# Low halves of three first projections, and differences of neighbouring tokens, on VectorE instead of GpSimd

## The chip, the cores and the metric

The kernel runs on one core of one Trainium2 chip. The metric is the device time of one execution in microseconds (us). Before the change it was 2815.28 us, the median of 3 runs (2813.53 to 2815.95).

Five engines work side by side, each through a queue of its own in order: TensorE (PE in the profile; its weight loads are PEld), VectorE (DVE), ScalarE (ACT), GpSimd (POOL) and SyncE (SP), which here issues nearly all transfers (DMA).

## The reference

A trunk of two layers on 1024 tokens of width 1024, in float32. Layer 0 is windowed and dilated attention with a gated MLP; layer 1 is an RWKV-7 time mix with a gated MLP. The change lies at the start of the time mix:

```python
xx = jnp.pad(h[:, :-1], ((0, 0), (1, 0), (0, 0))) - h
xr, xw, xk, xv, xa, xg = [h + xx * mu[i] for i in range(6)]
r = xr @ w_rkv[0]
k = xk @ w_rkv[1]
v = xv @ w_rkv[2]
w = -jax.nn.softplus(-(w0 + jnp.tanh(xw @ w1) @ w2)) - 0.5
...
a = jax.nn.sigmoid(a0 + (xa @ a1) @ a2)
g = jax.nn.sigmoid(xg @ g1) @ g2
```

`xx` is the difference between a token and the one before it, the six `x?` are the mixes. Decay `w`, rate `a` and gate `g` each go through a narrow first projection (`w1`, `a1`, `g1`) and a second one.

## The kernel before, in words

**Two halves of a number.** PE multiplies in a rounded type, fp32r. To keep float32 accuracy every operand is split: the high half is the operand cast to fp32r (ACT), the low half is the operand minus its high half (a subtraction). A product is then three matmuls: high by high, high by low, low by high (`mm3`, lines 180 to 182). `split` (line 154) does cast and subtraction, the subtraction on DVE unless it is told otherwise.

**Tiling.** Tokens go in two halves of 512 (the loop over `q` in `rwkv_dense`), the 1024 channels in 8 blocks of 128 partitions (`k`). A tile is 128 channels by 512 tokens. `hT[k]` holds the normed activations, channels on partitions, with one column more at the front for the token before.

**The stage that the change touches.** For each half:

- line 1144 makes the 8 differences `xx` from two shifted views of `hT[k]`: for even `k` on DVE, for odd `k` on POOL;
- `mix` (line 1149) makes a mixed tile on DVE with one instruction, `xx * mu + h`;
- `mixed` makes the mixes for values (`xv`), receptance (`xr`) and keys (`xk`) and splits them with `split`: tiles `xi`, both halves by ACT and DVE;
- `lora1` does a first projection. It loads its weights (`lw`), splits them (lines 1176 and 1177), and then for each `k` makes a mix into a tile `s`, `u` or `sq` (DVE), casts it (line 1187, ACT) and makes the low half (line 1188, POOL), into a ring of three slots: two under the tag `tm` (`xl` in the profile) and one under `na`. Then come its matmuls into `pg` (gate) or `psi` (decay, rate). Gate comes first, then decay, then rate: 24 mixes per half;
- in the same loop over `ch` and `k` the value product runs: weights `wv` are loaded (`raw`), split (`wh` on ACT, `wl` on DVE; in half 1 `wl` comes back from DRAM, line 170), and multiplied with `xv` into `pv`. So the first projections are woven into the value product, three steps of `lora1` for two of `k`;
- then the gate's `rb` is finished (ACT, POOL, DVE), `pv` is copied to `u` and `sq` and stored (`v_d`), the second weights are split (`w`, `a`, `g2s`), the gate's second projection runs (`pz`, line 1286, stored as `gT`), and a loop over 8 blocks of columns `c` makes keys and receptance and all that follows from them.

The tag `tm` is also used at the end of that loop over `c`, for tiles that are stored as `bm_d` and `km_d`; so the first `xl` of half 1 wait for the last of these stores.

**What sets the order.** The order of instructions within a queue isn't that of the code. The kernel is built with

```python
with tile.TileContext(nc, schedule_with_timeline_sim=True) as tc:
```

which plans the order of every engine ahead of time from planned durations of its own. Once built, the order is fixed, and each engine takes its instructions strictly one behind the other; an instruction that waits for another engine holds up what is queued behind it. An edit that gives an instruction to another engine therefore also changes the planned order of others.

Of the kernel before, what the change touches and what calls it, by code (L numbers as in the profile page):

```python
# [11 lines left out]
F32 = mybir.dt.float32  # L12
# [7 lines left out]
ADD, SUB, MUL, MAX = ALU.add, ALU.subtract, ALU.mult, ALU.max  # L20
# [7 lines left out]
H = 512  # L28
# [1022 lines left out]
def rwkv_dense(t, hp, sv, hT, first):  # L1051

    tc, nc, a, dp = t.tc, t.nc, t.a, t.dp
    ve, ac, po, pe = nc.vector, nc.scalar, nc.gpsimd, nc.tensor
# [81 lines left out]
    for q in range(2):  # L1136
# [4 lines left out]
        for k in range(NK):  # L1141
            if k % 2 == 0:
                x2 = (sv, sv, up, up)[k // 2].tile([P, 2, H], F32, name="xx", tag=("n", "ub", "bk", "ar")[k // 2], bufs=(1, 1, 2, 2)[k // 2])
            (po if k % 2 else ve).tensor_tensor(x2[:, k % 2], hT[k][:, q * H:(q + 1) * H], hT[k][:, 1 + q * H:1 + (q + 1) * H], SUB)
            xx.append(x2[:, k % 2])

        def mix(i, k, tag):
            x = tile_(tag)
            ve.scalar_tensor_tensor(x, xx[k], t.v(f"mu{i}", k), hT[k][:, 1 + q * H:1 + (q + 1) * H], MUL, ADD)
            return x  # L1150
# [8 lines left out]
        def lora1(i, name, halves, *parts):  # L1159

            n = a[name].shape[1] // NK
            per = (256 if name == "a1" else 512) // n
            raw = wp.tile([P, NK * n], F32, name="lw", tag="lw", bufs=1)
            nc.sync.dma_start(raw, a[name])
            raw = raw.rearrange("p (k c) -> p k c", k=NK)
            ws = []  # L1170
            for k0 in range(0, NK, per):
                kn = min(per, NK - k0)
                w = next(halves)[:, :kn * 2 * n].rearrange("p (k c) -> p k c", k=kn)
                for c0, m, _ in parts:
                    src, wh, wl = raw[:, k0:k0 + kn, c0:c0 + m], w[:, :, 2 * c0:2 * c0 + m], w[:, :, 2 * c0 + m:2 * c0 + 2 * m]
                    ac.copy(wh, src)
                    ve.tensor_tensor(wl, src, wh.bitcast(F32), SUB)
                ws += [w[:, k] for k in range(kn)]
            for k in range(NK):
                x = mix(i, k, ("s", "u", "sq")[k % 3])  # L1180
                tag = next(rings)
                if tag == "tm":
                    xs = tp.tile([P, 2, H], F32R, name="xl", tag=tag)
                    xs = xs[:, 0], xs[:, 1]
                else:
                    xs = [tile_(tag, dt=F32R) for _ in range(2)]
                ac.copy(xs[0], x)
                po.tensor_tensor(xs[1], x, xs[0].bitcast(F32), SUB)
                for c0, m, ps in parts:
                    w = ws[k][:, 2 * c0:2 * c0 + 2 * m]  # L1190
                    if m > 64:
                        t.mm3(ps, w[:, :m], w[:, m:], *xs, k == 0, k == NK - 1)
                    else:
                        for j in (0, 1) if k == 0 else (1, 0):
                            mj = m if j else 2 * m
                            pe.matmul(ps[:mj], w[:, :mj], xs[j], start=k == j == 0, stop=k == NK - 1 and not j)
                yield

        def product(i, xi, c):
            wh, wl = t.load_split(wp, a["wrk"][i, c], D, "w", 2, lo=po if i == 0 and not q else ve, **through(wrkl[i, c]))  # L1200
            ps = pm.tile([P, H], F32, name="pz", tag="mm")
            for k in range(NK):
# [11 lines left out]
        a1s = (tile_("xx", dt=F32R) for _ in range(2))  # L1214
        rings = itertools.cycle(["tm", "tm", "na"])
        parts = itertools.chain(lora1(5, "g1", slots, (0, P, pga), (P, 32, pgb)),
                                lora1(1, "w1", w1s, (0, 64, psw)), lora1(4, "a1", a1s, (0, 64, psa)))
        xrs = []
        for ch in range(2):
# [437 lines left out]
def trunk(tc, a, out):  # L1657
    with ExitStack() as ctx:
        t = Trunk(ctx, tc, a, out)
        x_m, x_d, x_l = (t.dp.tile([T, D], F32, name=n) for n in ("x_m", "x_d", "x_l"))  # L1660
        hp = ctx_pool(tc, "hp", "left")
        mp = ctx_pool(tc, "mp", "left")
        o, merge = t.attention(hp.pool, mp.pool)
        up = t.ffn_up(0, "left", "right")
        mt = ctx_pool(tc, "mt", "left")
        r = t.out_proj("right", o, a["wout"], a["x"], x_m, None, 0, functools.partial(merge, mt.pool),
                       lambda: (mt.close(), mp.close(), next(up), next(up)))
        act = up.send((*r, hp))
        hp = ctx_pool(tc, "hr", "left")
        rn = ctx_pool(tc, "rn", "left", 2)  # L1670
        hT, done = rwkv_norm(t, hp.pool, rn.pool, x_d)
        t.ffn_down(0, act, x_m, "right", done)
        rn.close()
        sv = ctx_pool(tc, "sv", "right")
        d, scan, last = rwkv_dense(t, hp, sv.pool, hT, Scan)
        o, op, behind = rwkv_scan(t, d, scan, sv, last)
        scan.lp.close()
        ow = ctx_pool(tc, "ow", "right")
        up = t.ffn_up(1, "right", "left")
        next(up)  # L1680
        r = t.out_proj("left", o, a["wo"], x_d, x_l, ow, 1, None, lambda: next(up), behind)
        act = up.send((*r, op, ow))
        zn = ctx_pool(tc, "zn", "right", 2)
        t.ffn_down(1, act, x_l, "left", t.final(zn.pool))
        zn.close()
# [23 lines left out]
```

## Time and profile before

| what | value |
| --- | --- |
| median of 3 runs | 2815.28 us |
| the profiled execution's own time | 2819.46 us |
| its span (first to last instruction) | 2817.7 us |
| mean granted TensorE clock | 0.963 |
| differences `xx` (line 1144), DVE x8, median | 977 ns |
| differences `xx` (line 1144), POOL x8, median | 1453 ns |
| low halves (line 1188), POOL | 48 instructions, medians by group 1340 to 1750 ns |
| mixes (line 1149), DVE | 96 instructions, medians by group 740 to 751 ns, longest 2367 ns |
| first low half starts, half 0 and half 1 | 1289.9 us, 1567.5 us |
| last low half starts, half 0 and half 1 | 1364.9 us, 1629.1 us |

The profile is of one execution. A row of its timeline has the start in us from the start of the span, the duration, the engine, the line of the kernel, the operation and what it writes and reads; in brackets how long the engine idled before it and which instruction released it. In a view of groups a row is one line with one operation and shape: its count, the time it was busy, the mean duration in ns, and the idle time before its instructions with what ended it. In a view of waits a row reads "A <- B: total us, times, longest": A waited until B was done. Instructions on DVE overlap a little, so the next starts some 0.08 us before the end that is shown for the one ahead.

### The profile page before, as it was taken

What the parts mean: (1) busy time and instruction counts of PE and PEld (TensorE: products, weight loads), DVE (VectorE), ACT (ScalarE), POOL (GpSimd) and SP (SyncE); (2) the same over time, 40 slices, a digit from 0 to 9 for tenths busy, and PEclk for the clock granted to TensorE, in tenths of its full rate; (3) what the DMA queues carried; (4) which work ended last, traced back from release to release, by engine and by line L of the source; (5) the groups of instructions that cost most, each with busy time, mean ns of one, the idle gap of its engine ahead of it and who ended that gap; (6) DMA issues with size and microseconds to landing.
All of it is one profiled execution on the core that took longest, in us unless ns stands there. A gap on an engine that the chain in (4) does not pass through costs nothing.

```text
span 2817.7 us, 42321 instructions
## 1 busy us (share of the span) xinstructions
PE 2648.6 (94%) x15526; PEld 2117.2 (75%) x15526; DVE 1739.9 (62%) x2961; ACT 1198.0 (43%) x2387; POOL 1053.6 (37%) x768
## 2 busy tenths in 40 slices
PE   8999998989999999998899889889899999999998
PEld 7777776677888877776677657678877888887776
DVE  4555565566344447888767677766677544444988
ACT  3445446334333333355644454334434333333334
POOL 1221221236434425545444433224444534441644
PEclk9999999999999999999999999888899999999999
DMA  4111112632222237463667588898552322225654
GB/s 140 46 38 46 46 53 73 216 111 82 83 86 86 79 115 254 152 202 112 215 201 206 148 245 214 216 253 247 180 195 86 105 79 87 79 69 204 206 157 161
DMA packets 304751, 392.61 MB, mean 139 GB/s; under 512 B 97928, under 2 KB 167944, under 8 KB 304544
## 3 DMA queue, kind: packets, MB, share of 16 engines
q1 hardware_dynamic: 299568, 375.72, 42.6%
q10 hardware_dynamic: 4496, 12.62, 1.1%
q8 instruction: 122, 2.00, 0.3%
q0 software_dynamic: 480, 1.57, 0.2%
q14 instruction: 85, 0.70, 0.1%
HBM read 281.56 MB, written 108.27 MB: 138 GB/s over the span
## 4 chain that ended last, share of the span: by engine, by line
PE 55%; DVE 14%; DMA 6%; issue 3%; POOL 2%; ACT 1%; SPq 1%; POOLq 0%; DVEq 0%; ACTq 0%
PE y L784 17%; PE z L784 9%; PE pd L932 6%; PE x L784 4%; PE pg L1360 2%; DVE ws L154 2%; DVE as L154 2%; PE pz L180 2%; PE pz L182 2%; PE pz L181 2%; PE o L1474 2%; DMA raw<-in_wd 2%; PE po L180 2%; PE po L181 1%; PE po L182 1%
## 5 line engine op out<-in xcount | busy, mean ns | idle before, releaser
L932 PE MATMUL pd<-ws,as 128*128 128x512 f32 x1848 | 431.9, 395 | 21.4 <-DVE ws L154 20.3
L932 PEld LDWEIGHTS pd<-ws,as 128*128 128x128 f32 x1848 | 350.7, 191 | 100.6 <-DVE ws L154 25.4
L784 PE MATMUL y<-t,cw 128*128 128x512 f32 x1584 | 370.2, 389 | 0.0
L784 PEld LDWEIGHTS y<-t,cw 128*128 128x128 f32 x1584 | 297.3, 188 | 62.4
L154 DVE TENSOR_TENSOR cw<-raw,cw 128x512 fp32r<-128x512 f32 x264 | 213.5, 811 | 201.6 <-ACT cw L154 198.0
L154 ACT CAST cw<-raw 128x512 fp32r<-128x512 f32 x264 | 163.1, 621 | 245.8 <-PE z L784 103.8
L793 POOL TENSOR_TENSOR c<-c 128x512 f32<-128x512 f32 x66 | 111.7, 1692 | 187.7 <-DVE c L800 136.7
L154 ACT CAST wh<-raw 128x512 fp32r<-128x512 f32 (+1 forms) x122 | 93.3, 766 | 173.5 <-PE mm L181 53.6
L180 PE MATMUL mm<-hx,wh 128*128 128x512 f32 x384 | 163.8, 427 | 0.0
L154 DVE TENSOR_TENSOR wl<-raw,wh 128x512 fp32r<-128x512 f32 (+1 forms) x114 | 110.4, 970 | 84.4 <-ACT wh L154 81.6
L788 ACT COPY sn<-y 128x512 f32<-128x512 f32 x132 | 76.9, 586 | 196.4 <-PE y L784 193.1
L182 PE MATMUL mm<-hx,wl 128*128 128x512 f32 x384 | 152.3, 397 | 0.0
L181 PE MATMUL mm<-hx,wh 128*128 128x512 f32 x384 | 151.6, 395 | 0.0
L784 PE MATMUL z<-b,cw 128*128 128x512 f32 x576 | 142.8, 399 | 6.6 <-DVE tx L730 6.6
L784 PEld LDWEIGHTS z<-b,cw 128*128 128x128 f32 x576 | 111.0, 193 | 31.1 <-issue 7.0
L154 ACT CAST as<-raw 128x512 fp32r<-128x512 f32 x110 | 68.2, 620 | 153.7 <-PE pd L932 80.1
L264 POOL TENSOR_TENSOR ry<-ry,S 128x512 f32<-128x512 f32 x40 | 51.7, 1293 | 217.3 <-DVE ry L263 192.8
L784 PE MATMUL y<-b,cw 128*128 128x512 f32 x528 | 129.0, 394 | 0.0
L784 PE MATMUL z<-t,cw 128*128 128x512 f32 x528 | 123.4, 389 | 0.0
L784 PE MATMUL x<-b,cw 128*128 128x512 f32 x480 | 116.4, 397 | 0.0
L784 PEld LDWEIGHTS y<-b,cw 128*128 128x128 f32 x528 | 98.8, 187 | 22.7
L826 POOL TENSOR_TENSOR raw<-s,raw 128x512 f32<-128x512 f32 x44 | 58.9, 1339 | 151.9 <-DVE cw L154 151.7
(464 smaller groups left out, 6091.8 us busy)
## 6 DMA issues: line engine op xcount, KB each, us to landing
raw<-act SPq DMA_DIRECT2D x132, 256.0 KB, 3.1
raw<-in_wd SPq DMA_DIRECT2D x132, 256.0 KB, 2.9
raw<-in_wg SPq DMA_DIRECT2D x88, 256.0 KB, 2.7
raw<-in_wu SPq DMA_DIRECT2D x88, 256.0 KB, 2.7
act<-c SPq DMA_DIRECT2D x88, 256.0 KB, 2.0
raw<-in_wrk SPq DMA_DIRECT2D x32, 512.0 KB, 4.8
raw<-in_win SPq DMA_DIRECT2D x24, 512.0 KB, 3.5
raw<-in_wout SPq DMA_DIRECT2D x32, 256.0 KB, 3.5
```

The lines of the kernel that those rows point to most:

```text
L154: return self.nc.scalar.copy(hi, src), (eng or self.nc.vector).tensor_tensor(lo, src, hi.bitcast(F32), SUB)
L180: seen(mm(ps, lh, rh, start=start, stop=False))
L181: seen(mm(ps, lh, rl, start=False, stop=False))
L182: seen(mm(ps, ll, rh, start=False, stop=stop))
L264: nc.gpsimd.tensor_tensor(y, y, self.S[:, s], MUL)
L784: seen(pe.matmul(ps, w[:, x, s], bs[:, k, y], start=start and k == j == 0, stop=k == 3 and j == 2, skip_group_check=True))
L788: ac.copy(s, ps)
L793: po.tensor_tensor(g, g, u, MUL)
L826: po.tensor_tensor(a11, s, a11, SUB)
L932: pe(ps[b], s[:, x, t], w[:, y], start=first and i == 0, stop=f == N - 1 and i == 2, skip_group_check=True)
L1360: pe.matmul(ps[:, i], bk[rows, h * 4 + i].rearrange("p x t -> p (x t)"), ar[rows, h * 4 + i].rearrange("p y t -> p (y t)"), start=True, st ...
L1474: own(pe.matmul(*x, **k, skip_group_check=True))
```

## The change

Two words change: `po` (GpSimd) becomes `ve` (VectorE).

```diff
@@ -1141,7 +1141,7 @@
         for k in range(NK):
             if k % 2 == 0:
                 x2 = (sv, sv, up, up)[k // 2].tile([P, 2, H], F32, name="xx", tag=("n", "ub", "bk", "ar")[k // 2], bufs=(1, 1, 2, 2)[k // 2])
-            (po if k % 2 else ve).tensor_tensor(x2[:, k % 2], hT[k][:, q * H:(q + 1) * H], hT[k][:, 1 + q * H:1 + (q + 1) * H], SUB)
+            ve.tensor_tensor(x2[:, k % 2], hT[k][:, q * H:(q + 1) * H], hT[k][:, 1 + q * H:1 + (q + 1) * H], SUB)
             xx.append(x2[:, k % 2])
@@ -1185,7 +1185,7 @@
                 ac.copy(xs[0], x)
-                po.tensor_tensor(xs[1], x, xs[0].bitcast(F32), SUB)
+                ve.tensor_tensor(xs[1], x, xs[0].bitcast(F32), SUB)
                 for c0, m, ps in parts:
```

Per half of the tokens, 24 subtractions of `lora1` (the low halves) and 4 differences (`xx` of the odd `k`) go from POOL's queue to DVE's: 48 and 8 in all. The arithmetic is the same. Both halves of every other split stay where they were, and so do the first split of the receptance weights in half 0 and the gate's `rb` on POOL.

The order within the queues moves with it. On DVE, at the first low halves of half 0 (tiles: `xi` low half of a mix for the values or receptance, `wl` low half of the value weights, `s`, `u`, `sq` mixes for the first projections or for receptance). Before:

```order
L154 TENSOR_TENSOR xi<-xx,xi 128x512
L154 TENSOR_TENSOR wl<-raw,wh 128x512
L1149 SCALAR_TENSOR_TENSOR s<-xx,vec,hT_8537 128x512
L1149 SCALAR_TENSOR_TENSOR u<-xx,vec,hT_8541 128x512
L1149 SCALAR_TENSOR_TENSOR xx<-xx,vec,hT_8538 128x512
L1149 SCALAR_TENSOR_TENSOR sq<-xx,vec,hT_8536 128x512
```

Behind six mixes (`s`, `u`, `sq` twice) one `xi` and one `wl` are made, and then four further mixes. On DVE at the same place, from the fourth of the six mixes on, in the changed kernel:

```order
L1149 SCALAR_TENSOR_TENSOR s<-xx,vec,hT_8534 128x512
L1149 SCALAR_TENSOR_TENSOR u<-xx,vec,hT_8538 128x512
L1149 SCALAR_TENSOR_TENSOR sq<-xx,vec,hT_8539 128x512
L154 TENSOR_TENSOR wl<-raw,wh 128x512
L154 TENSOR_TENSOR xi<-xx,xi 128x512
L154 TENSOR_TENSOR wl<-raw,wh 128x512
L1188 TENSOR_TENSOR xl<-s,xl 128x512
L1188 TENSOR_TENSOR xl<-u,xl 128x512
L1188 TENSOR_TENSOR na<-sq,na 128x512
L1149 SCALAR_TENSOR_TENSOR xx<-xx,vec,hT_8538 128x512
```

Three low halves of the gate's projection now stand together in DVE's queue, ahead of the next mix, and one `wl` more ahead of them.

On DVE again, at the end of the stage in half 0, around `g2s` (part of the gate's second weights, which PE needs to begin the second half of each gate product); `s` and `xi` are here the mixes for the keys and their low halves, `r` and `il` belong to decay and rate. Before:

```order
L1263 TENSOR_TENSOR a_11338<-raw,a_11338 64x1024
L154 TENSOR_TENSOR xi<-s,xi 128x512
L154 TENSOR_TENSOR wl<-raw,wh 128x1024
L1149 SCALAR_TENSOR_TENSOR s<-xx,vec,hT_8537 128x512
L154 TENSOR_TENSOR xi<-s,xi 128x512
L1144 TENSOR_TENSOR xx<-hT_8536 128x512
L1253 TENSOR_TENSOR r<-r,psi 64x512
L1149 SCALAR_TENSOR_TENSOR s<-xx,vec,hT_8538 128x512
L154 TENSOR_TENSOR xi<-s,xi 128x512
L1281 TENSOR_TENSOR g2s<-raw,g2s 32x1024
```

In the changed kernel, from the same split of the rate's second weights (`a`):

```order
L1263 TENSOR_TENSOR a_11338<-raw,a_11338 64x1024
L1188 TENSOR_TENSOR xl<-s,xl 128x512
L1266 TENSOR_TENSOR il<-r,xx 64x512
L1188 TENSOR_TENSOR na<-u,na 128x512
L1149 SCALAR_TENSOR_TENSOR s<-xx,vec,hT_8534 128x512
L154 TENSOR_TENSOR xi<-s,xi 128x512
L154 TENSOR_TENSOR wl<-raw,wh 128x1024
L1149 SCALAR_TENSOR_TENSOR s<-xx,vec,hT_8535 128x512
L1281 TENSOR_TENSOR g2s<-raw,g2s 32x1024
L1144 TENSOR_TENSOR xx<-hT_8534 128x512
L1144 TENSOR_TENSOR xx<-hT_8535 128x512
```

The mixes for the keys now begin behind the last low halves, and `g2s` stands behind the second of them (`hT_8535`) instead of the fifth (`hT_8538`); the differences of half 1 follow it in pairs. From here on to the end of the loops over columns the other queues are also planned anew, with the same instructions.

## The prediction

> **What bounds the kernel now.** The page comes first: TensorE (PE) is busy nearly all the time, so only the stages in which PE waits can give anything.
>
> ```profile
> span 2817.7 us, 42321 instructions
> PE 2648.6 (94%) x15526; PEld 2117.2 (75%) x15526; DVE 1739.9 (62%) x2961; ACT 1198.0 (43%) x2387; POOL 1053.6 (37%) x768
> ```
>
> The instructions that the change touches lie in two stretches, one for each half of the tokens. The view of busy time by stretch (columns: stretch, its length, busy PE, PEld, DVE, ACT, POOL with counts, granted clock, DMA share, GB/s) sets them side by side. The first runs from the first mix of half 0 to the last split of its mixes for the keys, the second from the first low half of half 1 to the start of its loop over columns.
>
> ```profile
> 1280.00:1383.30 103.30, 84.75 (x323) 61.23 (x324) 96.99 (x115) 62.07 (x109) 49.97 (x30) 0.88 0.40 134
> 1574.00:1646.90 72.90, 58.69 (x205) 40.18 (x205) 61.45 (x67) 46.39 (x79) 41.95 (x31) 0.87 0.51 156
> ```
>
> In the first VectorE (DVE) is busy 96.99 of 103.30 us and PE idles 18.6: DVE bounds it. In the second DVE is busy 61.45 of 72.90 and PE idles 14.2; there DVE and transfers take turns. Next the timeline of DVE, then of GpSimd (POOL), at the first low halves (start, duration, instruction):
>
> ```profile
> 1289.76 0.74 DVE L1149 SCALAR_TENSOR_TENSOR sq<-xx,vec,hT 128x512 f32<-128x512 f32 x1
> ...
> 1294.89 1.77 DVE L1149 SCALAR_TENSOR_TENSOR s<-xx,vec,hT 128x512 f32<-128x512 f32 x1 [1.19 <-POOL xl L1188]
> 1296.58 1.78 DVE L1149 SCALAR_TENSOR_TENSOR u<-xx,vec,hT 128x512 f32<-128x512 f32 x1
> ...
> 1299.61 0.68 DVE L154 TENSOR_TENSOR wl<-raw,wh 128x512 fp32r<-128x512 f32 x1
> 1300.21 0.68 DVE L154 TENSOR_TENSOR xi<-s,xi 128x512 fp32r<-128x512 f32 x1
> ```
>
> ```profile
> 1294.80 1.30 POOL L1188 TENSOR_TENSOR xl<-u,xl 128x512 fp32r<-128x512 f32 x1
> 1296.05 1.76 POOL L1188 TENSOR_TENSOR na<-sq,na 128x512 fp32r<-128x512 f32 x1
> ```
>
> The same mix takes 0.74 us with POOL still and 1.77 or 1.78 beside a POOL subtraction; a DVE subtraction takes 0.68, and the next starts 0.60 after it. So a POOL low half is not free for DVE: it costs up to 1.03 us of its queue, while the same subtraction on DVE costs 0.60. What ends PE's waits, first stretch, then second (total, times, longest):
>
> ```profile
> PE pv L181 <- DVE wl L154: 6.0, 4, 2.6
> PE pz L1286 <- DVE g2s L1281: 3.8, 1, 3.8
> PE psi L1196 <- POOL na L1188: 2.7, 2, 2.4
> ```
>
> ```profile
> PE pg L180 <- ACT xl L1187: 5.0, 1, 5.0
> PE pv L180 <- ACT wh L171: 3.3, 1, 3.3
> PE pz L1286 <- DVE g2s L1281: 3.0, 1, 3.0
> PE pz L182 <- DVE wl L154: 1.0, 1, 1.0
> ```
>
> ```profile
> ACT rb L1237 <- DVE an L154: 3.3, 1, 3.3
> ```
>
> PE mostly waits for DVE or POOL. The 3.3 us for ScalarE's (ACT's) `wh` are DVE's too: `wh` stood in ACT's queue behind `rb`, which waited 3.3 us for DVE. Only the 5.0 us come from elsewhere (below).
>
> **The change part by part.** *Removed from DVE: the stretching.* Groups of DVE instructions of the first stretch, shapes kept apart (count, busy us, mean ns, idle before):
>
> ```profile
> L1149 DVE SCALAR_TENSOR_TENSOR s<-xx,vec,hT 128x512 f32<-128x512 f32 x25 | 27.8, 1115 | 1.4 <-POOL xl L1188 1.2
> L154 DVE TENSOR_TENSOR xi<-s,xi 128x512 fp32r<-128x512 f32 x16 | 13.7, 860 | 1.9 <-ACT xi L154 1.7
> L154 DVE TENSOR_TENSOR wl<-raw,wh 128x512 fp32r<-128x512 f32 x14 | 12.2, 871 | 0.3 <-ACT wh L154 0.3
> L1149 DVE SCALAR_TENSOR_TENSOR u<-xx,vec,hT 128x512 f32<-128x512 f32 x9 | 7.7, 858 | 1.6 <-DMA v_d<-u 1.6
> L1149 DVE SCALAR_TENSOR_TENSOR xx<-xx,vec,hT 128x512 f32<-128x512 f32 x8 | 6.9, 869 | 0.0
> L1149 DVE SCALAR_TENSOR_TENSOR sq<-xx,vec,hT 128x512 f32<-128x512 f32 x6 | 6.6, 1097 | 0.0
> ...
> L1144 DVE TENSOR_TENSOR xx<-hT 128x512 f32<-128x512 f32 x3 | 3.9, 1284 | 0.0
> ...
> L1266 DVE TENSOR_TENSOR il<-r,xx 64x512 fp32r<-64x512 f32 x2 | 2.2, 1104 | 0.0
> ```
>
> 48 mixes took 49.0 us; at 0.74 they are 35.5: 13.5 us of stretching. At 0.68 each the 16 `xi` hold 2.8, the 14 `wl` 2.7, the three `xx` 1.9, the two `il` 0.8. Together 21.7 us, and with the 1.2 us in which DVE waited for POOL 22.9. The second stretch:
>
> ```profile
> L1149 DVE SCALAR_TENSOR_TENSOR s<-xx,vec,hT 128x512 f32<-128x512 f32 x22 | 25.6, 1176 | 8.2 <-POOL xl L1188 7.9
> L154 DVE TENSOR_TENSOR xi<-s,xi 128x512 fp32r<-128x512 f32 x15 | 13.8, 919 | 1.6 <-ACT xi L154 1.6
> L1149 DVE SCALAR_TENSOR_TENSOR u<-xx,vec,hT 128x512 f32<-128x512 f32 x7 | 7.3, 1037 | 1.6 <-POOL xl L1188 1.6
> L1149 DVE SCALAR_TENSOR_TENSOR sq<-xx,vec,hT 128x512 f32<-128x512 f32 x3 | 3.2, 1083 | 1.1 <-DMA v_d<-sq 1.1
> L1266 DVE TENSOR_TENSOR il<-r,xx 64x512 fp32r<-64x512 f32 x2 | 2.4, 1220 | 0.0
> L1263 DVE TENSOR_TENSOR a<-raw,a 64x1024 fp32r<-64x1024 f32 x1 | 2.2, 2206 | 0.0
> ```
>
> In the same way 9.3, 3.6, 2.1, 1.0 and 1.0, and about 1.0 on `a` if twice 0.60 is taken for its 1024 columns: 18.0 us. Of DVE's waits for POOL I count 1.2 of the 7.9 and the 1.6; the remaining 6.7 is one wait that stands behind a transfer, the next point. So 20.8 us.
>
> *Added to DVE.* 24 low halves in each half of the tokens, at the 0.60 us pitch 14.4. Of the differences, four of half 0 and four of half 1 move. Two stand right ahead of the first stretch and two at its end, 2.4 us; two lie ahead of it, before PE has ended the stage before, and two in half 1 where PE still has matmuls: none of those four is counted. Should that cover be gone, they cost 2.4 us more. First stretch: +16.8 - 22.9 = -6.1. Second: +14.4 - 20.8 = -6.4.
>
> *Added waits.* A low half must follow ACT's cast of the same mix, and now holds up DVE's queue, not POOL's: behind it stand mixes that ACT waits for and `wl` and `xi` that PE waits for. The nearest rows are `xi` and `wl`, which follow a cast in the same way: 2.0 us for 30 of them in the first stretch, 0.07 each, so 24 cost 1.6 us a half. I take that, since the planned order puts eight other instructions between a mix and its low half at the start. Above it the bound is what POOL itself waits for these casts (last term of the rivals); below, nothing.
>
> *Moved.* The moved instructions issue no transfers, so SP's queue gets nothing new. POOL keeps `rs_r`, the two gate `rb` and the memsets, which no longer queue behind low halves. The `g2s` that PE waited 3.8 and 3.0 us for stands earlier among the mixes for the keys, which shortens that wait but lengthens the one for the last key mix: nothing is counted. The planner has also reordered all engines after this stage, with the same work; I take nothing for it, and 5 us either way in the range, about the longest single wait quoted (5.0).
>
> *What does not move.* Chain of waits in the second stretch, its longest transfers (start, duration):
>
> ```profile
> 1572.01 4.46 DMA km_d<-tm
> 1589.32 4.06 DMA v_d<-sq
> ...
> 1619.24 4.25 DMA raw<-in_g
> 1638.19 6.10 DMA gT<-u
> ```
>
> The cast into `xl` shares its buffers with `tm`, whose store `km_d` lands at 1576.5: the 5.0 us of PE and the 6.7 of DVE stay.
>
> *Sum:* -6.1 - 6.4 + 1.6 + 1.6 = -9.3 us. The profiled execution took 2819.46 us, 4.18 above the median of 2815.28. It becomes 2810.2, and with the same offset the median becomes **2806.0**.
>
> One rule of the Trainium skill bears on the row of 0.74 against 1.77: its page "SBUF — State Buffer", section "Who interferes with whom", says that a VectorE instruction with two inputs in SBUF and a GpSimd instruction that reads SBUF exclude each other for a whole instruction. The trace agrees in kind. If each of the 48 held DVE for its full unhindered 1.30 us, the sum would be 48 x (0.60 - 1.30) = -33.6 us; I keep the row sums, since DVE's own instruction overlaps part of POOL's and POOL loses time as well.
>
> **The rivals.** *More goes than DVE's own time:* PE's quoted waits for DVE or POOL vanish, 6.0 + 3.8 + 2.7 and 3.3 + 3.0 + 1.0 = 19.8 us, giving 2795.5. For it: a cast, a low half and a mix chase each other over three queues, now over two. Against: DVE still has about 92 us of work (96.99 - 21.7 + 16.8) in the first stretch.
>
> *Nothing to be measured:* the second stretch goes from transfer to transfer (4.46, 4.06, 4.25, 6.10), and a faster DVE only waits longer at each; the first stretch keeps half of its 6.1 because low halves wait. Then about -3: 2812.
>
> *Slower:* low halves at the head of DVE's queue. What POOL waited for their casts (first stretch, then a window around the second):
>
> ```profile
> POOL xl L1188 <- ACT xl L1187: 28.5, 10, 4.9
> ```
>
> ```profile
> POOL xl L1188 <- ACT xl L1187: 21.4, 9, 6.2
> ```
>
> On POOL nobody stood behind those 49.9 us. If DVE inherits half, 25 against 12.5 saved make +12.5: 2827.8. It decides from a quarter on, 12.5 us. For it: `xl` and `na` have few buffers, a cast waits until PE has read the tile before, and PE waits for `wl`, which is now behind. Against: the planner ordered DVE anew with these waits in its plan, and the 30 `xi` and `wl` hardly wait.
>
> *The change gives no relief:* DVE's long instructions come from something other than POOL. Then the saturated first stretch grows by 16.8 us, and the second by 14.4 less its 11.45 idle us, together about 20: 2835. Against it, short and long rows of the same form alternate with POOL's instructions. In the Trainium skill this is the advice of "Perfetto Trace Analysis", section "Optimizing Scalar/DVE Operations", that a saturated VectorE may be helped by moving work to GpSimd; the same place adds that the two share a read port, so that it might not help.
>
> **How the numbers follow.** Forecast 0.53 (its own range 2799 to 2809), more 0.13, nothing 0.20, slower 0.10, no relief 0.04. A measurement of this kernel tells about 0.2%, 5.6 us, from no change: faster is under 2809.7, slower above 2820.9. The first two cases are faster, 0.66; the third the same, 0.20; the last two slower, 0.14. The range goes from 2791, below the second case by some of the 5 us for the reordering, to 2821, the edge of the third case with it; outside are most of the last two and a little of the second.
>
> **What would show it.** Right: no L1188 on POOL; the mixes `s` at a mean of 0.75 us, not 1.12 or 1.18; the low halves on DVE at 0.68; the first stretch shorter by 4 to 6 us with DVE still busy nine tenths of it, the second by about 5; PE's waits for `wl` and `na` smaller. Wrong: waits of DVE's L1188 for ACT's L1187 over 6 us a half, or `s` rows still above 1 us, or both stretches shorter and the time given back after 1650 us.

## The result, and the profile after

The changed kernel takes 2805.74 us (median of 8 runs, 2797.55 to 2807.51). The kernel before, run again beside it, has a median of 2819.63 us over 8 runs. The ratio is **0.9948, 95% interval 0.9931 to 0.9964**, or 14.7 us less. The forecast of 2806.0 against 2815.28 is a ratio of 0.9967: the direction holds, and the gain is about 5 us larger than forecast. That the time itself lies 0.3 us from 2806.0 is luck: the kernel before came out 4 us higher this time, and the gain came out larger. In several of the measurements below a single execution took far longer than all others of its kernel (here one of before, 3272.75 us); such executions are left out of the ratios.

The profiled execution took 2802.01 us. The head of its page:

```profile
span 2800.2 us, 42294 instructions
PE 2647.3 (95%) x15526; PEld 2120.7 (76%) x15526; DVE 1723.4 (62%) x3017; ACT 1198.6 (43%) x2387; POOL 964.0 (34%) x712
```

DVE has 56 instructions more, POOL 56 fewer, and DVE is busy 16.5 us *less*: what it gave up in stretching is more than what it took over. PE's busy time is the same.

To see where the 17.45 us between the two profiled executions lie, I cut both at the same instructions of PE: the first value product (`pv`), the first product of the loop over columns (line 1299) in half 0, the same in half 1, the first matmul of the last MLP (line 784), and the end. The view of busy time by stretch gives one row for each piece (stretch, length, busy PE with its count, PEld, DVE, ACT, POOL, granted clock, DMA share, GB/s). Before:

```profile
1281.63:1383.72 102.09, 85.17 (x324) 61.56 (x325) 95.36 (x111) 60.86 (x106) 49.97 (x30) 0.88 0.40 134
1383.72:1645.01 261.29, 240.05 (x1203) 180.97 (x1201) 179.21 (x252) 130.93 (x234) 116.39 (x91) 0.94 0.66 199
1645.01:2144.20 499.19, 458.65 (x5130) 380.18 (x5131) 339.09 (x710) 200.97 (x413) 165.72 (x116) 0.90 0.75 214
2144.20:2817.70 673.50, 646.75 (x2805) 527.80 (x2803) 397.30 (x487) 261.72 (x457) 296.86 (x203) 0.98 0.37 124
```

After:

```profile
1281.56:1364.95 83.39, 79.10 (x324) 59.51 (x325) 79.38 (x126) 55.56 (x98) 9.58 (x4) 0.92 0.48 156
1364.95:1624.98 260.03, 243.01 (x1201) 182.66 (x1201) 173.13 (x277) 132.41 (x237) 74.38 (x61) 0.93 0.66 200
1624.98:2123.40 498.42, 457.71 (x5131) 380.86 (x5131) 345.99 (x725) 205.42 (x418) 166.39 (x120) 0.89 0.75 216
2123.40:2800.20 676.80, 647.54 (x2805) 528.93 (x2803) 396.44 (x487) 261.82 (x457) 294.55 (x203) 0.98 0.36 123
```

The counts of PE agree to one or two, so each pair holds the same matmuls. In these two executions the whole gain stands in the first piece: -18.7 us, of which 12.6 are idle time of PE (16.92 to 4.29) and 6.1 are the same 324 matmuls taking less time, at a granted clock of 0.92 instead of 0.88. The second piece, in which half 1's low halves lie, is only 1.3 us shorter, the third 0.8. The last, where nothing was changed, is 3.3 longer; a piece of a single execution is uncertain by at least that much.

DVE's groups in the first piece (count, busy us, mean ns, idle before):

```profile
L1149 DVE SCALAR_TENSOR_TENSOR s<-xx,vec,hT 128x512 f32<-128x512 f32 x21 | 15.6, 745 | 0.0
L154 DVE TENSOR_TENSOR wl<-raw,wh 128x512 fp32r<-128x512 f32 x14 | 9.6, 684 | 0.6 <-ACT wh L154 0.6
L154 DVE TENSOR_TENSOR xi<-s,xi 128x512 fp32r<-128x512 f32 x10 | 6.8, 684 | 0.0
L1188 DVE TENSOR_TENSOR xl<-s,xl 128x512 fp32r<-128x512 f32 x6 | 4.1, 687 | 0.0
```

The means of 1115, 871 and 860 ns have become 745, 684 and 684: up to the start of the loop over columns no instruction of these groups is stretched any more. The next two mixes, beside the one split of the receptance weights that stayed on POOL (2.99 us from 1367.57), take 3.56 us together. What ends PE's waits, first stretch, then second:

```profile
PE pv L180 <- ACT xi L154: 3.8, 1, 3.8
PE psi L1196 <- DVE xl L1188: 1.8, 1, 1.8
...
PE pv L181 <- DVE wl L154: 0.5, 1, 0.5
PE psi L1196 <- DVE na L1188: 0.5, 1, 0.5
```

```profile
PE pg L180 <- ACT xl L1187: 3.5, 1, 3.5
PE prn L1328 <- DVE rb L1325: 1.9, 1, 1.9
PE psi L1196 <- DVE xl L1188: 1.6, 2, 1.4
```

Of the waits shown before, 6.0 us for `wl` have become 0.5, and both waits for `g2s` (3.8 and 3.0) are gone. The 3.8 us for `xi` end where the first piece begins (before: 2.9). The wait for `xl` in half 1 is still there. DVE's own waits for the casts, first in half 0, then in half 1:

```profile
DVE xl L1188 <- ACT xl L1187: 0.3, 1, 0.3
```

```profile
DVE xl L1188 <- ACT xl L1187: 8.5, 6, 5.8
...
DVE na L1188 <- DMA nk_d<-na: 0.7, 1, 0.7
```

So DVE did not inherit POOL's 49.9 us of waits. The one long wait, 5.8 us, is the one for the store `km_d`: ACT's cast ahead of it waited for that store (2.1 us). All the same, 8.5 us is above the 6 us a half that the prediction had named as a sign of being wrong; without that one wait, which it expected to stay, 2.7 are left.

### The profile page after: what moved, and what is told of

The parts are those of the page before. It is cut to its first block, busy times and chain, and to the rows that moved or that the text cites. A ratio compares the mean times of both kernels' runs of the same rounds, so it can differ in the third digit from the quotient of the medians.

```text
span 2800.2 us, 42294 instructions
## 1 busy us (share of the span) xinstructions
PE 2647.3 (95%) x15526; PEld 2120.7 (76%) x15526; DVE 1723.4 (62%) x3017; ACT 1198.6 (43%) x2387; POOL 964.0 (34%) x712
## 4 chain that ended last, share of the span: by engine, by line
PE 56%; DVE 12%; DMA 7%; issue 3%; ACT 2%; POOL 2%; SPq 1%; DVEq 0%; POOLq 0%; ACTq 0%
PE y L784 17%; PE z L784 9%; PE pd L932 6%; PE x L784 4%; PE o L1474 2%; DVE ws L154 2%; PE pg L1360 2%; DMA raw<-in_wd 2%; DVE as L154 2%; PE po L180 2%; PE po L181 2%; PE pz L180 2%; PE po L182 2%; PE pz L182 1%; PE pz L181 1%
## 5 line engine op out<-in xcount | busy, mean ns | idle before, releaser
L800 DVE TENSOR_TENSOR c<-z,sn 128x512 f32<-128x512 f32 x92 | 63.4, 689 | 85.2 <-ACT sn L788 74.8
```

The source lines that it names most:

```text
L800: ve.tensor_tensor(c[-1], z, s, ADD)
```

## The experiments

Four theories. **Sharing**: GpSimd's subtractions stretch VectorE's instructions, and VectorE's queue sets the pace. **Chain**: the gain is one queue less between a cast and its matmuls. **Differences**: the eight differences stand at the head of every product and were late. **Order**: the planner's new order makes the gain, whatever engine does the work.

### Each edit alone

```diff
-                po.tensor_tensor(xs[1], x, xs[0].bitcast(F32), SUB)
+                ve.tensor_tensor(xs[1], x, xs[0].bitcast(F32), SUB)
```

> Only the 48 low halves go to VectorE; the differences stay divided between VectorE and GpSimd. Sharing (theory: GpSimd's subtractions stretch VectorE's instructions, and VectorE's queue bounds both stretches): 48 of the 56 moved instructions are here, so about 48/56 of the 0.52% that both edits gave, a ratio to the kernel before of 0.9955 (0.994 to 0.997); mixes s at about 0.75 us except beside the two GpSimd differences at the end of the first stretch. Differences (rival: the mixes of every product start from xx, so the eight differences on GpSimd are what was late): under a third of it, 0.998 or above. Order (rival: the gain is the planner's new order, not the engine): the order of VectorE differs here from the changed kernel's in over 1000 lines, so the ratio can be anything from 0.99 to 1.005 and the parts need not add up.

Measured: 0.9976 (0.9962 to 0.9989), -6.8 us. The other edit alone:

```diff
-            (po if k % 2 else ve).tensor_tensor(x2[:, k % 2], hT[k][:, q * H:(q + 1) * H], hT[k][:, 1 + q * H:1 + (q + 1) * H], SUB)
+            ve.tensor_tensor(x2[:, k % 2], hT[k][:, q * H:(q + 1) * H], hT[k][:, 1 + q * H:1 + (q + 1) * H], SUB)
```

> Only the eight odd differences go to VectorE; the 48 low halves stay on GpSimd. Sharing: 8 of 56, and four of them lie where TensorE isn't waiting: 0.9995 (0.998 to 1.001). Differences: most of the gain, 0.995 to 0.997. Order: anything; not the complement of the kernel with the low halves alone.

Measured: 0.9970 (0.9960 to 0.9979), -8.4 us. The two add up to the whole (-15.2 against -14.7), but they are not divided as sharing had it: its two values are missed, and the theory of the differences had the second one right. Which of the two gives more isn't settled, though: the intervals overlap, and by the medians alone (2808.97 and 2811.11 against 2817.81) the low halves lead. The pieces of the profile speak for the low halves. First two pieces with the low halves alone, then with the differences alone:

```profile
1285.06:1369.20 84.14, 76.49 (x324) 58.10 (x325) 81.42 (x127) 58.07 (x101) 13.70 (x6) 0.96 0.48 156
1369.20:1628.57 259.37, 239.98 (x1202) 180.03 (x1200) 171.28 (x278) 133.30 (x237) 77.74 (x67) 0.94 0.68 202
```

```profile
1280.71:1377.57 96.86, 81.31 (x325) 58.62 (x325) 90.94 (x108) 57.59 (x101) 44.63 (x28) 0.93 0.42 136
1377.57:1645.55 267.98, 248.66 (x1202) 184.98 (x1202) 173.31 (x259) 133.60 (x239) 107.83 (x89) 0.91 0.65 196
```

From the first value product to the loop of half 1 the low halves alone take 343.5 us, the changed kernel 343.4, the kernel before 363.4: in this stage of these executions they make all of the gain. The differences alone take 364.8: nothing. Their profiled execution took 2819.27 us, 8 above their own median, so its later pieces cannot be used to find the 8.4 us.

### The differences, divided

```diff
-            (po if k % 2 else ve).tensor_tensor(x2[:, k % 2], hT[k][:, q * H:(q + 1) * H], hT[k][:, 1 + q * H:1 + (q + 1) * H], SUB)
+            (po if k % 2 and q else ve).tensor_tensor(x2[:, k % 2], hT[k][:, q * H:(q + 1) * H], hT[k][:, 1 + q * H:1 + (q + 1) * H], SUB)
```

> Only the four odd differences of the first half of the tokens go to VectorE; everything else as before. All eight gave 0.9970, which 8 of 56 moved instructions don't explain. Sharing at the head: two of the four lie ahead of the first mixes at 1276 to 1279 us and delay VectorE by up to 1.0 us each: 0.9995. Order: these four change 887 lines of VectorE's order, those of the second half 392; if the order makes the gain, most of the 0.30% is here, 0.998 or less.

Measured: 1.0022 (1.0007 to 1.0036), 6 us slower. With `not q` in place of `q`:

> Only the four odd differences of the second half of the tokens go to VectorE. Sharing at the end of the first stretch: GpSimd's difference there waited 4.4 us for VectorE, and three VectorE instructions of about 0.7 us took 1.5 to 1.75 us beside the two of them; 4 to 5 us of the 8.4 that all eight gave: 0.9983 (0.997 to 0.9995). Order: under 0.1%, the rest being with the first half.

Measured: 0.9985 (0.9967 to 1.0002), as sharing expected, but not clear of 1. The sum of the two is +0.07%, both together -0.30%. So the theory of the differences falls too: what they bring is no sum of parts, and no theory here had a slower kernel for the first four. Why they slow it stays open.

### Order alone

The mixes take other tiles in turn, which changes no instruction's engine or size:

```diff
-                x = mix(i, k, ("s", "u", "sq")[k % 3])
+                x = mix(i, k, ("u", "sq", "s")[k % 3])
```

> The kernel before with the mixes of the first projections taking their tiles in the order u, sq, s instead of s, u, sq: no instruction changes its engine or its size, but the planner writes 829 lines of VectorE's order anew. Sharing alone: 1.000 (0.999 to 1.001). Order (the planned order is worth some us by itself, as the pair of kernels with half of the differences each suggests, which came out at 1.0022 and 0.9985 where both together gave 0.9970): away from 1 by 0.15% or more, either way.

Measured: 1.0000 (0.9983 to 1.0016). The other kernel of this kind:

```diff
-        rings = itertools.cycle(["tm", "tm", "na"])
+        rings = itertools.cycle(["na", "tm", "tm"])
```

> The kernel before with the ring of buffers for the halves of the first projections' mixes begun at na instead of tm: again no instruction changes its engine or size; 863 lines of VectorE's order differ, and the first halves of the second half of the tokens no longer land in the buffer whose store ends last. Sharing alone: 0.999 to 1.001, or 0.998 if the 5.0 us that TensorE waits for that store go. Order: away from 1 by 0.15% or more, either way.

Measured: 1.0001 (0.9987 to 1.0014). Two new orders of over 800 lines each are worth nothing that can be measured in total, though they move time between pieces: with the second, the first piece takes 96.96 us, 5.1 less than before, just as with the differences alone, and the total is the same. In it `g2s` stands behind the third mix for the keys instead of the fifth, and PE waits 1.5 us for it instead of 3.8. So the place of `g2s`, which the planner also moved in the changed kernel, can shorten the first piece without any instruction changing its engine; by itself it did not shorten the whole. The change under the first of these orders:

> The changed kernel with the same tiles order u, sq, s: the same change under another planned order (1121 lines of VectorE's). Sharing: its ratio to the kernel with that order and without the change is again about 0.995 (0.993 to 0.997), so 0.995 times whatever that kernel shows against before. Order only: the change has no effect of its own, and the two kernels with this order agree within 0.2%.

Measured: 0.9936 (0.9915 to 0.9957), median 2795.95 us, the lowest of all, though the interval overlaps that of the changed kernel. Its first two pieces:

```profile
1286.05:1372.84 86.79, 77.85 (x324) 58.75 (x325) 83.25 (x132) 58.24 (x101) 9.10 (x4) 0.95 0.46 151
1372.84:1621.23 248.39, 233.82 (x1202) 177.66 (x1200) 180.88 (x283) 133.14 (x238) 78.73 (x65) 0.97 0.70 212
```

335.2 us against 357.6 with that order and without the change: -22.4, where the first order gave -20.0. In this pair PE's wait for `g2s` hardly differs (2.0 and 1.7 us), and the first piece still goes from 102.41 to 86.79 us. The change holds its gain when the order is another one. Order as the cause falls; what it does to single pieces stays.

### GpSimd's reading, put back

The changed kernel with a subtraction on GpSimd beside each low half, whose result nobody uses:

```diff
                 ve.tensor_tensor(xs[1], x, xs[0].bitcast(F32), SUB)
+                po.tensor_tensor(tp.tile([P, H], F32, name="dup", tag="dup", bufs=1), xs[0].bitcast(F32), xs[0].bitcast(F32), SUB)
```

> The changed kernel, and beside each of its 48 low halves on VectorE an extra GpSimd subtraction of the old form (128x512, high half minus itself) into a scratch tile that nobody reads. Sharing: VectorE carries the added 48 x 0.60 us and is stretched again, so all of the gain goes and more: 21.7 + 18.0 us of stretching come back on a kernel that is 14.6 us faster than the one before: a ratio to before of about 1.004 (1.000 to 1.009), mixes s at a mean over 1 us. Chain (rival: the gain is one queue less between a cast and its matmuls, or the planner's order): the extra work is on nobody's path, 0.994 to 0.998, as without it.

Measured: 1.0069 (1.0049 to 1.0088), 34 us more than the changed kernel. The control writes and does not read (two memsets, tied to the same moment by a copy of one column on ScalarE):

```diff
                 ve.tensor_tensor(xs[1], x, xs[0].bitcast(F32), SUB)
+                dup = tp.tile([P, H], F32, name="dup", tag="dup", bufs=1)
+                ac.copy(dup[:, :1], xs[0][:, :1].bitcast(F32))
+                po.memset(dup, 0.0)
+                po.memset(dup, 1.0)
```

> The control to the kernel with the extra subtractions: two GpSimd memsets of 128x512 (about 0.52 us each) into the scratch tile in their place, which write SBUF and read nothing; a copy of one column on ScalarE ahead of them ties them to the same time. Sharing by reading: mixes stay at 0.75 us and the ratio to before stays that of the changed kernel, 0.994 to 0.997. Sharing by any access: mixes are stretched as by the subtractions, 1.000 or above. Chain: 0.994 to 0.998.

Measured: 0.9970 (0.9955 to 0.9986). The timelines of DVE and POOL with the subtractions:

```profile
1300.03 1.52 DVE L1149 SCALAR_TENSOR_TENSOR sq<-xx,vec,hT 128x512 f32<-128x512 f32 x1
1301.48 1.52 DVE L154 TENSOR_TENSOR xi<-xx,xi 128x512 fp32r<-128x512 f32 x1
1302.93 0.74 DVE L1149 SCALAR_TENSOR_TENSOR s<-xx,vec,hT 128x512 f32<-128x512 f32 x1
```

```profile
1299.72 2.74 POOL L1189 TENSOR_TENSOR dup<-xl 128x512 f32<-128x512 f32 x2 [2.69 <-ACT xl L1187]
```

Two subtractions, two long DVE instructions, and the next one is short again. The mixes `s` came to a mean of 0.92 us in the first stretch, not over 1 us: VectorE's new low halves took a share of the stretching. With the memsets, all mixes `s`, `u` and `sq` of the first stretch are short:

```profile
L1149 DVE SCALAR_TENSOR_TENSOR s<-xx,vec,hT 128x512 f32<-128x512 f32 x21 | 15.5, 745 | 0.0
...
L1149 DVE SCALAR_TENSOR_TENSOR u<-xx,vec,hT 128x512 f32<-128x512 f32 x9 | 6.7, 747 | 2.8 <-DMA v_d<-u 2.8
...
L1149 DVE SCALAR_TENSOR_TENSOR sq<-xx,vec,hT 128x512 f32<-128x512 f32 x6 | 4.5, 746 | 0.0
```

Sharing is shown, and by reading alone: 96 memsets of 0.53 us each leave DVE's instructions as they are, 48 subtractions that nobody waits for cost 34 us. Chain falls with it as the whole of the cause: no queue was put back between a cast and its matmuls, and more than the gain was lost. In the profile 25.8 of the 42.0 us between this execution and that of the changed kernel lie up to the loop of half 1 (1650.77 against 1624.98); 16.6 lie in the third piece, where no subtraction was added, and why they do is open. The Trainium skill, "SBUF — State Buffer", section "Who interferes with whom", says just this: a two-input VectorE instruction contends with a GpSimd instruction that reads SBUF, not with one that only writes it. Its other part (section "SBUF: two separate sides"), that whichever of the two starts first has the shared ports for the whole instruction, fits the rows less well: a subtraction of 1.37 us lengthens one DVE instruction by 0.78 to 0.84 (0.74 and 0.68 to 1.52). For DVE's queue that is 48 times 0.81, an estimate of 38.9 us, against 66 at the full 1.37. The 34 us of the whole kernel can't decide between them, since DVE's queue isn't all of its time.

### Each half of the tokens alone

Both edits, with the old division kept in half 1 (and for the second kernel in half 0, with `q` and `not q` exchanged):

```diff
-            (po if k % 2 else ve).tensor_tensor(x2[:, k % 2], hT[k][:, q * H:(q + 1) * H], hT[k][:, 1 + q * H:1 + (q + 1) * H], SUB)
+            (po if k % 2 and q else ve).tensor_tensor(x2[:, k % 2], hT[k][:, q * H:(q + 1) * H], hT[k][:, 1 + q * H:1 + (q + 1) * H], SUB)
...
-                po.tensor_tensor(xs[1], x, xs[0].bitcast(F32), SUB)
+                (po if q else ve).tensor_tensor(xs[1], x, xs[0].bitcast(F32), SUB)
```

> Both edits for the first half of the tokens only. In the traces TensorE's idle time from 1250 to 1400 us fell by 10.4 us, from 1575 to 1700 us by 6.3, and 3.8 were given back between and after. Sharing: the first half keeps its 10.4 less the 2.9 given back in the loop over columns behind it, so -7.5 us, a ratio of 0.9973 (0.996 to 0.9985), and with the other half alone it adds up to the whole, 0.9948. Order: since the second half is planned behind the first, the sum of the two halves misses the whole by more than 5 us.

Measured: 0.9973 (0.9962 to 0.9984), -7.6 us, as expected.

> Both edits for the second half of the tokens only. Sharing: TensorE's idle time from 1575 to 1700 us fell by 6.3 us and 0.9 were given back up to 1850 us: -5.4 us, a ratio of 0.9981 (0.997 to 0.9995). Order: the sum of the two halves misses the whole by more than 5 us.

Measured: 0.9988 (0.9976 to 1.0000), -3.4 us. The sum of -11.0 misses the whole by 3.7, within the intervals. The first two pieces, half 0 alone, then half 1 alone:

```profile
1285.01:1367.64 82.63, 76.90 (x324) 58.02 (x324) 79.82 (x126) 56.55 (x99) 13.15 (x6) 0.96 0.49 158
1367.64:1642.95 275.31, 248.13 (x1202) 186.20 (x1202) 183.94 (x263) 135.83 (x241) 115.17 (x91) 0.92 0.64 192
```

```profile
1283.51:1387.17 103.66, 83.74 (x324) 59.91 (x325) 94.76 (x113) 60.40 (x105) 47.40 (x28) 0.90 0.40 131
1387.17:1629.66 242.49, 232.37 (x1202) 176.15 (x1200) 168.86 (x264) 127.56 (x230) 75.12 (x61) 0.98 0.70 212
```

Alone, half 1 shortens its piece by 18.8 us, as much as half 0 its own (19.5). But neither reaches the total whole. With half 1 alone the profiled execution is only 8.1 us shorter than the one before (all that lies around the second piece takes 10.7 longer), and over all runs the gain is 3.4. With half 0 alone the second piece is 14.0 us longer, with the same 1202 matmuls busy 8.1 us longer at a clock of 0.92 for 0.94 and 6 us more of idle time, and the third is 11.4 shorter (487.75). So single pieces behind the first move by 10 us and more.

Read over all kept profiles that can be cut in this way, the first piece is the clear one: 82.4 to 86.8 us in the five kernels with half 0's low halves on VectorE, 96.8 to 104.3 in the seven with them on GpSimd. The second isn't: 242.5 to 266.0 in the five with half 1's low halves on VectorE, 255.2 to 275.3 in the others. What half 1 brings to the total is not shown to be more than the 3.4 us of its own measurement.

One place where time is lost in the second piece has a name. PE in the changed kernel, just into half 0's loop over columns:

```profile
1407.50 0.33 PE L1131 MATMUL pst<-cst,hs 128*128 128x128 f32 x1 [0.60 <-DVE hs L1129]
1409.48 0.49 PE L1299 MATMUL pz<-xx,w 128*128 128x512 f32 x1 [1.65 <-ACT an L1308]
```

The same wait of 1.65 us stands with half 0 alone, and not in the kernel before, with half 1 alone, or in the fastest kernel with its other order. What follows it, in the view by stretch:

```profile
1400.00:1410.00 10.00, 7.75 (x42) 5.67 (x40) 5.92 (x9) 4.33 (x6) 3.85 (x3) 1.00 0.80 263
1410.00:1420.00 10.00, 10.00 (x44) 8.20 (x45) 8.40 (x13) 3.83 (x7) 5.26 (x5) 0.53 0.51 161
1420.00:1430.00 10.00, 10.00 (x64) 7.21 (x63) 3.40 (x9) 4.34 (x10) 2.92 (x4) 0.96 0.25 65
```

Ten microseconds at a clock of 0.53 are 4.7 us of work lost, behind 2.25 us of waiting: some 7 us in the changed kernel. With half 0 alone the two slices behind the wait have clocks of 0.60 and 0.55, about 8.5 us of work, so that with the wait an estimated 11 of the 14 us lie here. It is one place and no rule: with the low halves alone this wait is missing, and their second piece is as long as the changed kernel's (259.37 us).

### The last subtractions moved as well

```diff
-            wh, wl = t.load_split(wp, a["wrk"][i, c], D, "w", 2, lo=po if i == 0 and not q else ve, **through(wrkl[i, c]))
+            wh, wl = t.load_split(wp, a["wrk"][i, c], D, "w", 2, **through(wrkl[i, c]))
```

> The changed kernel, and the last GpSimd subtractions near the stage go to VectorE too: the eight low halves wl of the receptance weights in the first half of the tokens (128x1024, 2.37 us each on GpSimd; 1.22 on VectorE). Only the first lies in the first stretch, where the mixes beside it took 3.56 us for two; the others lie in the loop over columns, where TensorE is busy all the time. Sharing: -1 to -3 us against the changed kernel, a ratio to before of 0.9942 (0.993 to 0.996). Order: within 0.3% of the changed kernel, either way.

Measured: 0.9986 (0.9968 to 1.0003), 0.38% slower than the changed kernel; both theories missed. Taking more reads off GpSimd was thus no further gain here. Its profiled execution was the fastest of its twelve (2804.41 us, the median is 2814.15), and in it the first two pieces take 348.4 us, 5 more than the changed kernel's, with the wait for `an` at 2.64 us instead of 1.65. Whether that wait is the cause stays open.

## Why the forecast was right, and where its terms were off

- **The cause** is shown: DVE was stretched by POOL's reading, and moving the subtractions took away more than it added. The control by reading and writing settles it against the chain as the whole cause, the other order against the planner. The size of the gain is not derived from it.
- **First stretch, forecast -6.1 + 1.6.** Its DVE side was right. Up to the last split of the mixes for the keys the stretch went from 103.30 us to 96.10 (-7.2):

```profile
1280.00:1376.10 96.10, 89.03 (x360) 66.14 (x361) 92.04 (x142) 65.52 (x114) 16.25 (x10) 0.93 0.52 172
```

  DVE's work fell from 96.99 to 92.04 us, as forecast (about 92). The forecast of -4.5 was 2.7 short because DVE's idle time fell too, from 6.3 to 4.1, instead of growing by 1.6 for new waits less 1.2 for old ones: DVE's new waits for the casts were 0.3.
- **"Nothing is counted" for `g2s`** was the step that failed, and with it the step from DVE's stretch to PE's time. PE's wait for `g2s` (3.8 us) went altogether, and PE began the loop over columns at 1364.95 instead of 1383.72: before, that was 0.4 us behind the end of the last split of a mix for the keys, now 11 us ahead of it. So PE gained 18.7 us where DVE's stretch became 7.2 shorter. Here the waits of PE told more than DVE's queue: the rival in which they vanish was right for `wl` and `g2s` in this half. For the total it was not: its -19.8 us is as far from -14.7 as the forecast's -9.3.
- **What the forecast had no term for** is PE's clock. 6.1 of the first piece's 18.7 us are the same matmuls at a higher clock. In slices of 10 us the kernel before has a clock under 1 in six of the eleven from 1280 to 1390 us (0.83, 0.83, 0.83, 0.74, 0.67, 0.91), the changed kernel in two (0.66 each).
- **Second stretch, forecast -6.4 + 1.6.** With half 1 alone its piece fell by 18.8 us, in the changed kernel by 1.3. The relief came (the mixes `s` and `u` of half 1 are at 745 ns too). DVE's new waits for the casts were 8.5 us; without the 5.8 for the store `km_d`, forecast to stay, 2.7 against the 1.6. That doesn't explain the missing gain: why so little of the 18.8 appears with both halves changed is known only for the one place above, and is open for the rest.
- **±5 us for the reordering** held for the total (two other orders: 1.0000 and 1.0001), but not for single pieces, which moved by 5 us and more.
- So -9.3 against about -14.7 is partly luck, the outcome of errors of opposite sign: 14 too little in the first stretch, 3.5 too much in the second, and some us in the pieces that one execution differs by. Of the signs named beforehand, the means of the mixes, DVE busy nine tenths of the first stretch and the smaller waits came; the first stretch became 7.2 us shorter and not 4 to 6, "the second by about 5" did not come, and one sign of being wrong, waits over 6 us in a half, came with the 8.5.
- **The rivals.** Waits inherited from POOL: 0.3 and 8.5 us, not 25. No relief: the mixes are at 745 ns. Nothing to be measured: the interval excludes 1.
- **Open:** why the differences alone give 0.30%, when their halves give -0.22% and +0.15%, and their profile shows no gain in the stage.

## What to carry to other kernels

Before work is put on GpSimd, ask what it reads beside a busy VectorE: here a subtraction of 1.37 us cost VectorE 0.8 us, more than the 0.60 that the same subtraction takes in VectorE's own queue. A saving in a stage that feeds TensorE is to be followed to the wait of TensorE that it ends, with any stretch at half clock behind it: shortening a queue by 7 us brought 19 there, and in the other half shortening it brought little to the total. The stage behind is to be looked at for a wait that the earlier start lays bare. Where a planner makes the order, time the change under a second order that changes nothing else; it tells cause from luck for the price of two kernels.

## What the runs showed of the hardware

**Two short waits were followed by a long stretch at half clock.** In the changed kernel, behind the waits of 0.60 and 1.65 us with one matmul of 0.33 us between them, the clock was 0.50 until about 1421 us:

```profile
1408.00:1410.00 2.00, 0.52 (x2) 0.29 (x2) 1.29 (x3) 0.98 (x2) 2.00 (x2) 1.00 0.61 186
1410.00:1412.00 2.00, 2.00 (x11) 1.96 (x12) 1.69 (x2) 1.75 (x3) 2.00 (x2) 0.63 0.01 2
...
1418.00:1420.00 2.00, 2.00 (x6) 1.61 (x6) 1.30 (x3) 0.55 (x1) 1.28 (x1) 0.50 0.48 150
1420.00:1422.00 2.00, 2.00 (x15) 1.23 (x17) 0.49 (x2) 0.62 (x2) 1.27 (x1) 0.81 0.37 112
```

The Trainium skill, "TensorE: Matmul & The Clock Gate", "Part 1", puts the fall to half rate after an idle window of about 3.4 us, and the return after about 3.4 us of work. The trace agrees in the half rate, not in the times: 2.25 us of waiting were enough, and some 10 us in which PE was shown busy passed before the clock came back. Much of that work was small products of 64 x 128 (line 1360); whether it was too light to bring the clock back sooner is not shown.

**GpSimd is slowed too.** In the changed kernel two of its instructions of one kind, beside a VectorE whose queue is full:

```profile
1318.68 0.97 POOL L1234 TENSOR_SCALAR rb<-rb 128x512 f32<-128x512 f32 x1 [32.73 <-ACT rb L1233]
1327.22 5.04 POOL L1240 TENSOR_SCALAR rb<-rb 32x512 f32<-32x512 f32 x1 [7.57 <-ACT rb L1239]
```

The smaller one took 5.04 us, and 3.19 in half 1, while DVE ran its own instructions at 0.60 to 0.67 us one behind the other; in the kernel before it took 0.99 and 1.05.

**A VectorE copy can be held for all of a GpSimd instruction.** In the loop over columns DVE's copy into `rb` has a median of 427 ns; beside POOL's subtraction into `wl` it takes 2.58 us, about as long as that one (2.35), and an earlier one 2.60 beside 2.38:

```profile
1410.35 2.58 DVE L1325 COPY rb<-rn 128x512 f32<-128x512 f32 x1 [0.31 <-POOL rn L1323]
```
